# The last gate product of a transformer block, computed without two experts and completed by their own results

## The chip, the cores and the metric

The kernel runs on one core of a Trainium2 chip, in float32 throughout. The metric is the device time of one execution in microseconds; of several, the median. A core has five engines with an instruction queue each: PE (TensorE, matrix products), DVE (VectorE), ACT (ScalarE), POOL (GpSimd) and SP, which here issues nearly all transfers. Products land in PSUM banks (128 partitions x 512 floats, eight of them), from where DVE or ACT reads them.

## The reference, cut to what matters

Three layers follow each other: one with sparse attention, then two of the second block (a dense one, and one with eight experts). The change is in the last of them only. There `h` holds 256 tokens x 1024, and the tokens' router has picked two experts of eight for each:

```python
out = zeros(256, 1024)                     # the mixture of experts, e = 0..7
for e in range(8):
    out = out + combine[:, e:e+1] * ((silu(f @ w1[e]) * (f @ w3[e])) @ w2[e])
h = h + out                                # w1, w3: 1024 x 3584, w2: 3584 x 1024
gate = sigmoid(rmsnorm(h, ple_norm_g[1]) @ ple_gate_w[1])       # 1024 x 1024
h = h + gate * (p[1] @ ple_proj_w[1])                           # p: 256 x 256
```

`rmsnorm(h, g)` is h / sqrt(mean(h^2) + eps) * g. The factor of a row can therefore be applied behind the product with the gate's weights, and the product itself is linear in h.

## The kernel before, in words

Each expert has 128 places. A token that picked it stands in one of them, and the rows of a one-hot matrix (`places`, `gather`) bring its activations there, turned so that the 1024 inputs lie on partitions (`xT`). The 3584 hidden columns are cut into four chunks (`CHUNKS`: 1024, 1024, 1024, 512). A step (e, c) in `STEPS` is one chunk of one expert: product w1 (silu behind it), product w3 (multiplied to it), and behind these w2 of the *previous* step, whose result (`ys`, places x 1024) is summed over the chunks. Experts go in pairs, (0, 4), (1, 5), (2, 6), (3, 7), and the two of a pair take turns chunk by chunk. Behind an expert's last chunk its `way_back` (one-hot, turned) and `scatter` multiply the results back onto tokens and add them to `h` with the gates.

`wide` (L1467) is every such product. Weights come in parts of 128 x 1024 floats (512 KB): eight for a product of 1024 columns, four for one of 512. The first 64 places are computed part by part as the weights come, two matmuls of 64 columns side by side on PE's array for each (in the trace four records of 128x512 a part, since a float32 matmul shows as two). The further places stand under `tc.If(many() > SET)` (L1492) and are computed only if the expert has more than 64 tokens. This branch, the reading of the second bank and the release of the parts are the `rest` of a product; it is run by `catch_up` after the *first* part of the product that follows, so that PE has work queued in front of it. `mids` are pieces of other work that are put between the parts.

`_Stream` holds one list of all weights in the order in which the program takes them. Each part that is released lets SP issue the next transfer into its slot (`load`, L93). In the stage with experts there are 32 slots: 8 `raw` of pool wp, 4 `wh`, 4 `wl`, 10 `raw` of qp and 6 of rp.

At the end stand: w2(7,3), the value product p @ ple_proj_w, the scatter of expert 7 into h, the transposing of the normalised h, the test `most > CAP` (an expert with more than 128 tokens; then all experts are computed once more over a second set of places by `overflow`, which loads its weights itself), and the gate product `ple` for two token tiles of 128. Its weights are split into a high and a low part (ACT L316, DVE L320, POOL L318: `wh`, `wl`) and multiplied in three passes; the last quarter of the columns is done in pieces of 256. SP stores each piece of h. `rows`, `P`, `D` = 128, 1024; `NT` = 2 token tiles, `KD` = 8 pieces of 128 inputs, `NE` = 8, `CAP` = 128.

Of the kernel before, what the change touches and what calls it, by code (L numbers as in the profile page):

```python
# [19 lines left out]
P = 128  # L20
# [28 lines left out]
STEPS = [(e, c) for e0 in range(NE // 2) for c in range(NC) for e in (e0, e0 + NE // 2)]  # L49
# [13 lines left out]
class _Stream:  # L63
# [3 lines left out]
    def __init__(self, net, plan):  # L67
        self.net, self.plan = net, plan
        self.parts = [(i, q, s) for i, c in enumerate(plan) for q, s in enumerate(c[4])]
        self.raw, self.got = {}, {}  # L70
        self.loaded = self.opened = self.cut = self.used = self.cur = self.first = self.live = 0
        self.slots, self.cap = [(net.wp, "raw", RAW)] * RAW, RAW
        self.extra, self.hold = set(), False

        self.last, self.keep = sum(len(c[4]) for c in plan[-3:]), None
# [17 lines left out]
    def load(self, between=None):  # L93
        while self.loaded < len(self.parts) and self.loaded < self.opened + self.cap:
            slot = self.slots.pop(0)
            if len(self.parts) - self.loaded <= self.last and slot[0] is not self.keep and slot[:2] != (self.net.wp, "raw"):
                self.cap -= 1
                continue
            self.slots.append(slot)
            pool, tag, n = slot  # L100
# [17 lines left out]
    def advance(self, n=PARTS):  # L118
        stop = self.cut + n
        while self.cut < stop and self.cut < len(self.parts) and self.live < PARTS:  # L120
# [4 lines left out]
            self.net.aid = {("p", 1): (1,), ("pg", 1, 0): (0, 1, 2, 3), ("pg", 1, 1): ()}.get(self.plan[i][0], self.net.aid)  # L125
# [44 lines left out]
class _Direct:  # L170


    def __init__(self, net, stream):
        self.net = net
        self.plan = {c[0]: c for c in stream.plan}
        self.slot = (net.qp, "raw", EARLY)
        assert stream.loaded == len(stream.parts) and len(stream.parts) - stream.used <= stream.last
# [7 lines left out]
    def get(self, j):  # L185
        if j not in self.got:
            k0, k1, c0, c1 = self.parts[j]
            pool, tag, n = self.slot
            v = self.net.t(pool, [P, 1024], tag, bufs=n).rearrange("p (k n) -> p k n", k=k1 - k0)
# [4 lines left out]
    def release(self, j):  # L194
        del self.got[j]


class _Net:
# [11 lines left out]
    def weights(self):  # L210
# [22 lines left out]
        for i in range(2):  # L233
# [16 lines left out]
            else:  # L250
# [8 lines left out]
                add(("p", 1), a["ple_proj_w_2"][1], 2, D, [(0, 2, 0, 512), (0, 2, 512, D)])  # L259
            for c in range(2):  # L260
# [1109 lines left out]
    def ple(self, i, xs, x1, r, pp, out=None):  # L1370
        nc = self.nc

        def done(c):
            cs = slice(c * 512, c * 512 + 512)

            def f(t, ps, ks=slice(0, 512)):
                sg = self.t(self.act, [P, D], "x", bufs=3)[:, 0:512]
                ds = slice(c * 512 + ks.start, c * 512 + ks.stop)
                nc.scalar.activation(sg[:, ks], ps[:, ks], AF.Sigmoid, scale=r[t])  # L1379
                nc.vector.tensor_mul(sg[:, ks], sg[:, ks], pp[t][:, ds])  # L1380
                nc.vector.tensor_add(self.h[:, t, ds], self.h[:, t, ds], sg[:, ks])  # L1381
                if out is not None:
                    nc.sync.dma_start(out[:, t, ds], self.h[:, t, ds])
# [5 lines left out]
        if out is None:  # L1389
            ps = self.banks("mm")  # L1390
            return self.join(self.groups(("pg", i, 1), ps, xs, done=lambda t: f(t, ps(t)), late=False))

        parts = self.ws.take(("pg", i, 1))
        for t, c0, c1 in ((0, 0, 512), (1, 0, 256), (1, 256, 512)):
            ps = self.bank("s" if c0 else "mm")
            for n, (j, (k0, _, _, _)) in enumerate(parts):
                self.passes(ps[:, c0:c1], xs[t], self.ws.get(j), k0, n == 0, n == len(parts) - 1, slice(c0, c1))
            f(t, ps, slice(c0, c1))
# [73 lines left out]
    def wide(self, key, outs, lhs, n, many, take, mids=None):  # L1472
# [4 lines left out]
        mids = mids or {}  # L1477
        parts = self.ws.take(key)
        end = parts[-1][1][1]

        def product(s, j, k0, k1):
            w = self.ws.get(j)
# [8 lines left out]
        def rest():  # L1491
# [6 lines left out]
            for j, _ in parts:  # L1498
                self.ws.release(j)
            take(1)  # L1500

        for i, (j, (k0, k1, _, _)) in enumerate(parts):
# [5 lines left out]
            if many is None:  # L1508
                product(1, j, k0, k1)
                product(2, j, k0, k1)  # L1510
                self.ws.release(j)
# [35 lines left out]
    def down(self, key, ys, g, n, many, first):  # L1547
# [3 lines left out]
        def lhs(s, k):  # L1551
            q, r = (n // 2 // P, SUB) if s else (n // P, SET)
            return g[:, int(s > 0), q * (s == 2) + k % q, r * (k // q) : r * (k // q) + r]

# [8 lines left out]
        self.wide(key, y, lhs, 512, many, take)  # L1563
# [4 lines left out]
    def scatter(self, t, e, back, ys, many=None):  # L1568

        ps = []  # L1570
        rows = [slice(SET * j, SET * j + SET) for j in range(2)]

        def first():
            ps[:] = [self.bank("tr") for _ in range(2)]
# [9 lines left out]

        def second():
# [5 lines left out]
            for j in range(2):  # L1591
                hv = self.h[:, t, j * 512 : j * 512 + 512]
                self.nc.vector.scalar_tensor_tensor(hv, ps[j], self.gates[:, t, e : e + 1], hv, ALU.mult, ALU.add)

        return first, second

    def experts(self, sp, p):
# [22 lines left out]
        for i, (e, c) in enumerate(STEPS):  # L1620
# [14 lines left out]
            if done is not None:  # L1635
                back[done], turn = self.way_back(sp, done)
                mids.setdefault(6, []).append(turn)
                late = {2 + 2 * t + k: [f] for t in range(NT) for k, f in enumerate(self.scatter(t, done, back[done], ys[done], F(number, done)))}
            if n < 512:
                assert not late  # L1640
# [8 lines left out]
        back[done], turn = self.way_back(sp, done)  # L1649
        turn()  # L1650
        hidden(*prev)
        for t in range(NT):
            for f in self.scatter(t, done, back[done], ys[done], F(number, done)):
                f()
        x = prev[0]
        back[x], turn = self.way_back(sp, x)
        turn()
        finish(*prev[:2])
        self.catch_up()
        return [f for t in range(NT) for f in self.scatter(t, x, back[x], ys[x], F(number, x))], pT  # L1660

    def overflow(self, sp, again):

        nc = self.nc
        most = nc.values_load(self.most[0:1, 0:1], min_val=0, max_val=S)
        with self.tc.If(most > CAP):
            self.ws, self.sets = _Direct(self, self.stream), {}
            for e in range(NE):
                oh, xT, ys = self.places(sp, e, CAP), self.inputs_T(), self.results()
# [4 lines left out]
                for c in range(NC):  # L1674
                    n = CHUNKS[c][1] // 2
                    s = self.t(sp, [P, 2, 512], "sw_s")
# [3 lines left out]
                for t in range(NT):  # L1680
                    for f in self.scatter(t, e, back, ys):
                        f()
            again()
            self.ws = self.stream

    def router_inputs(self):
# [4 lines left out]
        nc.gpsimd.memset(self.zeros, 0.0)  # L1691
        self.odd = self.t(self.fp, [P, 2], "odd")
# [5 lines left out]
    def route_join(self, gen):  # L1698
# [73 lines left out]
        self.next_gain()  # L1772
# [42 lines left out]
    def moe(self, i):  # L1815
        sp = self.se
        p = self.ple_load(i, self.act, "x", 3)
        done, pT = self.experts(sp, p)
        pp = [self.t(self.act, [P, D], "x", bufs=3) for t in range(NT)]
        value = self.ple_value(i, pT, pp)  # L1820
        x0, *x0T = (self.t(self.qp, [P, D], "raw", bufs=EARLY) for _ in range(3))
        x0T = [x.bitcast(F32R).rearrange("p (k n) -> p k n", k=KD) for x in x0T]
        self.play(value, n=2)
        done[0]()
        done[1]()
        self.scaled(0, x0)
        self.play(value, n=1)
        done[2]()
        done[3]()
        self.transposed(x0, x0T, 0, 4)  # L1830
        self.play(value)
        self.transposed(x0, x0T, 4, 8)
        self.overflow(sp, lambda: self.transposed(self.scaled(0, x0), x0T))
        xs = [x0T, self.new_xT()]
# [108 lines left out]
```

## Time and profile before

| | |
|---|---|
| three executions | 1772.24, 1764.77, 1763.61 us; median 1764.77 |
| the profiled execution, its span | 1774.91 us, 1773.1 us |
| PE, its weight loads | 1652.7 us (93%), 1014.6 us (57%) |
| DVE, ACT, POOL | 671.5 us (38%), 514.1 us (29%), 158.4 us (9%) |
| transfers | 491.70 MB, mean 277 GB/s; the hardware queue 72.1% of 16 engines' span |

Busy times are of the whole span, over stages with different limits; the stage of the experts takes roughly its second half. The profiled execution lies 10.1 us above the median, so differences are taken within it. In a timeline row `[5.17 <-PEq L1492]` says that the engine stood idle for 5.17 us ahead of this row, and that the last thing to end was its own sequencer at line 1492.

### The profile page before, as it was taken

How to read it: one execution, taken by the hardware profiler on the slowest of the kernel's cores; microseconds unless marked ns; L12 is line 12 of the kernel's file. 1: busy time of each engine (PE TensorE's matmuls, PEld its weight loads, DVE VectorE, ACT ScalarE, POOL GpSimd, SP SyncE). 2: the span in 40 equal slices, each digit the busy share in tenths (PEclk: the TensorE clock that was granted, in tenths of full speed). 3: DMA queues.
4: the chain of work that ended last, by engine and by line, in shares of the span. 5: the costliest groups of instructions: out<-in, count | busy, mean ns of one | idle time of the engine just before them, and what ended most of it. 6: DMA issues, size and time to landing. Idle time of an engine off the chain costs nothing. (4 is left out here: it accounts for less than half of the span.)

```text
span 1773.1 us, 24424 instructions
## 1 busy us (share of the span) xinstructions
PE 1652.7 (93%) x9746; PEld 1014.6 (57%) x9749; DVE 671.5 (38%) x1132; ACT 514.1 (29%) x840; POOL 158.4 (9%) x152
## 2 busy tenths in 40 slices
PE   8999989999999999999997999999999998998867
PEld 6887768777888877784332534336433344333336
DVE  6656767576445587571110130101120111311134
ACT  5646646555444455551100100000000001000013
POOL 2001432510000013500000000000000000000011
PEclk9999999999999999999999999999999999998979
DMA  8654335545555558567999998999789999999951
GB/s 272 201 175 146 108 95 168 180 122 185 182 187 190 190 163 292 194 250 308 406 407 399 400 393 306 406 357 401 283 320 374 408 397 404 370 407 407 397 207 38
DMA packets 176117, 491.70 MB, mean 277 GB/s; under 512 B 16670, under 2 KB 21206, under 8 KB 175920
## 3 DMA queue, kind: packets, MB, share of 16 engines
q1 hardware_dynamic: 171376, 474.28, 72.1%
q0 software_dynamic: 4544, 14.52, 2.8%
q8 instruction: 157, 2.57, 0.6%
q14 instruction: 40, 0.33, 0.0%
HBM read 486.60 MB, written 2.14 MB: 276 GB/s over the span
## 5 line engine op out<-in xcount | busy, mean ns | idle before, releaser
L272 PE MATMUL mm<-wh,xh 128*128 128x512 f32 (+4 forms) x888 | 324.0, 432 | 7.1 <-PEq L1492 4.0
L320 DVE TENSOR_TENSOR wl<-raw,wh 128x1024 fp32r<-128x1024 f32 x211 | 266.7, 1275 | 130.8 <-ACT wh L316 120.4
L272 PE MATMUL mm<-wh,xl 128*128 128x512 f32 (+1 forms) x704 | 281.4, 400 | 0.7 <-DVE xl L491 0.5
L316 ACT CAST wh<-raw 128x1024 fp32r<-128x1024 f32 x228 | 237.5, 1051 | 143.8 <-PE mm L272 68.2
L272 PE MATMUL mm<-wl,xh 128*128 128x512 f32 (+3 forms) x924 | 254.1, 416 | 1.2 <-DVE wl L320 0.6
L272 PE MATMUL mm<-raw,xh 128*64 128x512 f32 (+3 forms) x1388 | 201.2, 467 | 20.7 <-PEq L1492 14.2
L272 PE MATMUL o<-raw,sw_g 128*64 128x512 f32 (+1 forms) x1268 | 195.5, 503 | 16.7 <-PEq L1492 9.7
L272 PE MATMUL s<-raw,xh 128*64 128x512 f32 (+3 forms) x1432 | 193.4, 457 | 16.5 <-PEq L1492 12.4
L1532 DVE TENSOR_TENSOR sw_s<-sw_s,s 128x512 f32<-128x512 f32 (+1 forms) x64 | 39.8, 621 | 405.9 <-PE s L272 367.6
L272 PEld LDWEIGHTS mm<-wh,xh 128*128 128x128 f32 (+2 forms) x888 | 145.7, 180 | 54.4 <-issue 10.6
L272 PEld LDWEIGHTS mm<-wl,xh 128*128 128x128 f32 (+2 forms) x924 | 145.1, 175 | 51.5 <-issue 10.1
L272 PEld LDWEIGHTS mm<-wh,xl 128*128 128x128 f32 x704 | 134.9, 192 | 29.8 <-DVE xl L491 2.5
L318 POOL TENSOR_TENSOR wl<-raw,wh 128x1024 fp32r<-128x1024 f32 x17 | 43.0, 2549 | 1198.4 <-ACT wh L316 1178.4
L272 PEld LDWEIGHTS s<-raw,xh 128*64 128x64 f32 (+1 forms) x1432 | 77.0, 125 | 124.2 <-issue 80.9
L1544 ACT COPY sw_g<-tr 128x512 f32<-128x512 f32 (+1 forms) x32 | 17.1, 533 | 446.9 <-PE tr L275 425.8
L272 PEld LDWEIGHTS o<-raw,sw_g 128*64 128x64 f32 (+1 forms) x1268 | 72.0, 126 | 128.8 <-issue 95.8
L272 PEld LDWEIGHTS mm<-raw,xh 128*64 128x64 f32 (+1 forms) x1388 | 72.3, 127 | 119.0 <-issue 91.8
L1557 DVE TENSOR_TENSOR xl<-xl,o 128x512 f32<-128x512 f32 x48 | 33.0, 686 | 163.3 <-PE o L272 137.2
L1530 ACT ACTIVATE sw_s<-mm 128x512 f32<-128x512 f32 (+1 forms) x64 | 34.8, 544 | 206.0 <-PE mm L272 167.8
L272 PE MATMUL o<-wh,sw_g 128*128 128x512 f32 (+2 forms) x256 | 61.0, 488 | 3.8 <-PEq L1492 2.2
L272 PE MATMUL s<-wh,xh 128*64 128x512 f32 (+6 forms) x236 | 51.0, 467 | 3.3 <-PEq L1492 2.6
L275 PEld LDWEIGHTS tr<-c_ident,sw_s 128*128 128x128 f32 x280 | 34.0, 151 | 32.8 <-issue 9.1
(363 smaller groups left out, 1606.7 us busy)
## 6 DMA issues: line engine op xcount, KB each, us to landing
raw<-in_moe_w_dram SPq DMA_DIRECT2D x504, 512.0 KB, 10.2
raw<-in_dense_w_dram SPq DMA_DIRECT2D x84, 512.0 KB, 4.5
wh<-in_moe_w_dram SPq DMA_DIRECT2D x81, 512.0 KB, 10.2
wl<-in_moe_w_dram SPq DMA_DIRECT2D x80, 512.0 KB, 10.2
raw<-in_w_in_dram SPq DMA_DIRECT2D x48, 512.0 KB, 4.6
raw<-in_nsa_w_in_dram SPq DMA_DIRECT2D x44, 512.0 KB, 5.1
raw<-in_w_o_dram SPq DMA_DIRECT2D x16, 512.0 KB, 4.8
raw<-in_ple_gate_w_dram SPq DMA_DIRECT2D x16, 512.0 KB, 5.0
```

Of the source, the lines that this page charges most:

```text
L272: self.nc.tensor.matmul(out, lhsT, rhs, start=start, stop=stop, **kw)
L275: self.nc.tensor.transpose(out, in_, self.ident if ident is None else ident)
L316: self.nc.scalar.copy(wh, v)
L318: self.nc.gpsimd.tensor_tensor(wl, v, wh.bitcast(F32), ALU.subtract)
L320: self.owed.append(lambda: self.nc.vector.tensor_sub(wl, v, wh.bitcast(F32)))
L1530: nc.scalar.activation(s[:, i, :n], ps[i][:, :n], AF.Silu)
L1532: nc.vector.tensor_mul(s[:, i, :n], s[:, i, :n], ps[i][:, :n])
L1544: copy(g[:, i, : n // P, :], ps[:, :n].rearrange("p (q n) -> p q n", n=P))
L1557: self.nc.vector.tensor_add(ys[:, i, :], ys[:, i, :], y[i])
```

## The change

Seven things change, all in the last stage:

1. *Order.* In the last pair, the steps go (3,0), (3,1), (7,0), (3,2), (3,3), (7,1), (7,2), (7,3), so that expert 3 is done three steps before the end.
2. *The store.* From w1(3,1) on, the 16 slots outside pool wp are withdrawn as they come free. Thirteen of them take p, the two pieces of ple_proj_w, the eight of ple_gate_w, and two value tiles. 16 slots stay for experts' weights.
3. *The test for overflow* (with its second pass over all experts) stands behind w2(3,0), in step (3,1), instead of at the end.
4. *The gate product without experts 3 and 7.* At step (7,0) h holds experts 0, 1, 2, 4, 5, 6. It is turned and multiplied by the gain (`gate_inputs`), the value is computed (`value_T`, `value_part`), and in steps (3,2), (3,3) and (7,1) four `gate_part`s of eight full matmuls each fill `logit` (256 x 1024).
5. *The two experts' share.* The places' results of expert 3, and at the end of expert 7, are turned, multiplied by the gain (`result_T`), passed through the gate's weights in places' order (`result_logits`, a `wide` product over resident weights), and then scattered like results, but into `logit` as well as into h.
6. *The end:* w2(7,3), `result_T`, scatter into h, `result_logits`, the sums of squares of h and the factor of each row, then four quarters: scatter into the logits (DVE), sigmoid (ACT), times value (DVE), plus h (DVE), store.
7. The splitting of the gate's weights, and the three passes, fall away for this layer.

Cut to its core:

```diff
-STEPS = [(e, c) for e0 in range(NE // 2) for c in range(NC) for e in (e0, e0 + NE // 2)]
+STEPS = [(e, c) for e0 in range(NE // 2 - 1) for c in range(NC) for e in (e0, e0 + NE // 2)]
+LAST = len(STEPS)
+STEPS += [((NE // 2 - 1, NE - 1)[j], c) for j, c in ((0, 0), (0, 1), (1, 0), (0, 2), (0, 3), (1, 1), (1, 2), (1, 3))]
...
     def load(self, between=None):
         while self.loaded < len(self.parts) and self.loaded < self.opened + self.cap:
-            slot = self.slots.pop(0)
-            if len(self.parts) - self.loaded <= self.last and slot[0] is not self.keep and slot[:2] != (self.net.wp, "raw"):
+            pool, tag, n = slot = self.slots.pop(0)
+            if self.loaded >= self.grab_at and pool is not self.net.wp:
+                if self.grab:
+                    self.grab.pop(0)(self.net.t(pool, [P, 1024], tag, bufs=n))
                 self.cap -= 1
                 continue
...
+    def gate_part(self, t, c):
+        ps = self.bank("tr")
+        for k in range(KD):
+            self.mm(ps, self.hT[t][:, k, :], self.gate_w[k][:, c * 512 : c * 512 + 512], start=k == 0, stop=k == KD - 1)
+        self.nc.scalar.copy(self.logit[t][:, c * 512 : c * 512 + 512], ps)
...
+    def result_logits(self, g, zs, many):
+        def take(i):
+            if i:
+                self.nc.vector.tensor_copy(zs[:, i, :], z[i])
+            else:
+                self.nc.scalar.copy(zs[:, i, :], z[i])
+
+        z = self.set_banks("o")
+        self.ws = _Kept(self.gate_w)
+        self.wide("gate", z, self.turned_lhs(g, 512), 512, many, take)
+        self.ws = self.stream
...
+            if i == LAST + 2:
+                for j, (t, k0) in enumerate((t, k0) for t in range(NT) for k0 in (0, 4)):
+                    mids.setdefault(3 + j, []).append(F(self.gate_inputs, t, k0))
+                late = {1: [self.value_T]}
+                for j, (t, k) in enumerate((t, k) for t in range(NT) for k in range(2)):
+                    late[3 + j] = [F(self.value_part, t, k)]
+            if i == LAST + 3:
+                mids.setdefault(5, []).append(F(self.gate_part, 0, 0))
+                late = {4: [F(self.gate_part, 0, 1)]}
+            if i == LAST + 4:
+                late = {2: [F(self.gate_part, 1, 0)]}
+            if i == LAST + 5:
+                late = {4: [F(self.gate_part, 1, 1)]}
+            if i == LAST + 6:
+                for j in range(2):
+                    mids.setdefault(4 + j, []).append(F(self.result_T, ys[done], yT[0], j))
...
+            if i == LAST + 6:
+                self.result_logits(yT[0], zs, F(number, done))
             done = finish(*prev[:2]) if prev is not None else None
             prev = (e, c, s)
-            if i == len(STEPS) - 3:
-                pT = self.ple_T(p)
+            if i == LAST + 1:
+                self.catch_up()
+
+                x, y = self.inputs_T(), self.results()
+                self.overflow(sp, x, y)
...
+        finish(*prev[:2])
+        self.result_T(ys[e], yT[1], 0)
+        self.catch_up()
+        self.result_T(ys[e], yT[1], 1)
...
+        for f in scattered(ys[e], None):
+            f()
+        self.result_logits(yT[1], zs, many)
...
+        for t in range(NT):
+            self.halves(sq[:, t], t, junk)
+        r = self.rstd(sq)
+        self.catch_up()
+        for (t, j), f in zip(((t, j) for t in range(NT) for j in range(2)), scattered(zs, self.logit)):
+            f()
+            c = slice(j * 512, j * 512 + 512)
+            sg, hv = self.t(self.wp, [P, 1024], "wl", bufs=PARTS)[:, 0:512], self.h[:, t, c]
+            nc.scalar.activation(sg, self.logit[t][:, c], AF.Sigmoid, scale=r[:, t : t + 1])
+            nc.vector.tensor_mul(sg, sg, self.value[t][:, c])
+            nc.vector.tensor_add(hv, hv, sg)
+            nc.sync.dma_start(self.out[:, t, c], hv)
```

On SP, at the end of the list of weights, before: the last parts of the experts (`in_moe_w_2_dram`), behind them the projection and the gate's weights.

```order
L89 DMA raw_16281<-in_moe_w_2_dram 128x1024
L89 DMA wh_16283<-in_moe_w_2_dram 128x1024
L89 DMA raw_16551<-in_ple_proj_w_dram 128x2x512
L89 DMA raw_16646<-in_ple_proj_w_dram 128x2x512
L1589 UNCONDITIONAL_BRANCH
L89 DMA raw_16648<-in_ple_gate_w_dram 128x2x512
L1589 UNCONDITIONAL_BRANCH
L89 DMA raw_16650<-in_ple_gate_w_dram 128x2x512
```

On SP now, in the last steps of expert 6 and expert 3: the first four of these loads (L1674 is p, L1679 are rows of the two matrices) stand among the experts' parts (L92).

```order
L92 DMA wl_14032<-in_moe_w_2_dram 128x1024
L1496 UNCONDITIONAL_BRANCH
L92 DMA raw_14034<-in_moe_w_2_dram 128x1024
L1674 DMA raw_14149<-in_p_dram 128x2x256
L1679 DMA raw_14151<-in_ple_proj_w_dram 128x1024
L1679 DMA raw_14153<-in_ple_proj_w_dram 128x1024
L1679 DMA raw_14239<-in_ple_gate_w_dram 128x1024
L1679 DMA raw_14241<-in_ple_gate_w_dram 128x1024
L92 DMA raw_14243<-in_moe_w_2_dram 128x1024
```

The eleven loads moved from behind the last part of the experts to ahead of its last 144 parts.

On PE now, in product w3 of step (3,2): `s_6883` is the bank of the first 64 places, `wh` and `wl` are the experts' parts; the rows on `tr_25389` are a `gate_part` with the resident weights `raw_14239` to `raw_14548`.

```order
L1496 UNCONDITIONAL_BRANCH
L287 MATMUL s_6883<-wh_25245,xh_13949 64x512 x2
L287 MATMUL s_6883<-wh_25247,xh_13949 64x512 x2
L287 MATMUL s_6883<-wh_25249,xh_13949 64x512 x2
L287 MATMUL tr_25389<-raw_14239,xh_14995 128x512
L287 MATMUL tr_25389<-raw_14241,xh_14995 128x512
...
L287 MATMUL tr_25389<-raw_14548,xh_14995 128x512
L287 MATMUL s_6883<-wl_25251,xh_13949 64x512 x2
L287 MATMUL s_6883<-wl_25253,xh_13949 64x512 x2
```

Eight matmuls over all 128 tokens of a tile stand between two parts of an expert's product, whose release comes after them.

On DVE now, at the end: a sum of the factor's steps (`rms`), the copy of the second bank of `result_logits`, and of the four quarters the first two.

```order
L447 SCALAR_TENSOR_TENSOR rms_y_3239_27072<-rms_z_3238_27071,rms_y_3239_27072 128x2
L1658 COPY x_26136<-o_7222 128x512
L1781 UNCONDITIONAL_BRANCH
L1596 SCALAR_TENSOR_TENSOR x_24885<-tr_27151,gates_6842,x_24885 128x512
L1800 TENSOR_TENSOR wl_27177<-wl_27177,raw_14155 128x512
L1801 TENSOR_TENSOR h_85<-h_85,wl_27177 128x512
L1596 SCALAR_TENSOR_TENSOR x_24885<-tr_27152,gates_6842,x_24885 128x512
L1800 TENSOR_TENSOR wl_27183<-wl_27183,raw_14155 128x512
L1801 TENSOR_TENSOR h_85<-h_85,wl_27183 128x512
```

Each quarter's scatter add (L1596) stands behind the product and the add of the quarter ahead of it (L1800, L1801), of which the product waits for ACT's sigmoid.

## Rows read from the trace of the kernel before

**Rows 1.** Windows: core, busy time and records of each engine, granted clock, transfers.

```profile
core 0: us, PE busy (x) PEld busy (x) DVE busy (x) ACT busy (x) POOL busy (x), PEclk, DMA share, GB/s
1550.00:1598.00 48.00, 45.49 (x212) 17.18 (x210) 5.51 (x8) 4.73 (x8) 0.00 (x0) 1.00 1.03 407
1598.00:1704.00 106.00, 83.54 (x403) 34.78 (x399) 13.13 (x21) 6.64 (x13) 0.00 (x0) 0.89 1.02 397
1704.00:1726.00 22.00, 15.76 (x42) 6.16 (x40) 10.60 (x21) 3.21 (x4) 4.65 (x2) 0.60 0.23 83
```

**Rows 2.** Waits of the queue that issues weights: total us, times, longest.

```profile
SPq L89 <- DMA raw<-in_moe_w_dram: 90.7, 100, 1.5
```

**Rows 3.** Timeline of PE, 1560 to 1598 us: start, length, work, records, idle ahead.

```profile
1560.26 6.23 PE L272 MATMUL s<-raw,xh 128*64 128x512 f32 x28 [0.16 <-PEq L1492]
1575.12 1.06 PE L272 MATMUL mm<-raw,xh 128*64 128x512 f32 x4
1598.01 1.36 PE L272 MATMUL mm<-raw,xh 128*64 128x512 f32 x4
```

**Rows 4.** Timeline of PE, the long gaps of three steps after 1598 us.

```profile
1601.57 1.63 PE L272 MATMUL mm<-raw,xh 128*64 128x512 f32 x4 [2.19 <-PEq L1492]
1632.16 1.98 PE L272 MATMUL mm<-raw,xh 128*64 128x512 f32 x4 [5.14 <-PEq L1492]
1664.67 1.94 PE L275 MATMUL tr<-c_ident,sw_s 128*128 128x128 f32 x8 [5.17 <-PEq L1492]
```

**Rows 5.** Timeline of SP: last part of an expert, first gate weights.

```profile
1688.56 0.33 SPq L89 DMA_DIRECT2D wh<-in_moe_w_dram  x1
1694.66 33.88 SPq L89 DMA_DIRECT2D raw<-in_ple_gate_w_dram  x8
```

**Rows 6.** Transfers issued from 1550 us on: count, KB each, us to landing.

```profile
raw<-in_moe_w_dram SPq DMA_DIRECT2D x109, 512.0 KB, 10.2
```

**Rows 7.** Timeline of PE, from the last w2 on.

```profile
1720.45 4.96 PE L272 MATMUL o<-raw,sw_g 128*64 128x512 f32 x12
1725.24 1.02 PE L272 MATMUL o<-wh,sw_g 128*64 128x512 f32 x4
1740.84 0.49 PE L272 MATMUL mm<-wh,raw 128*128 128x512 f32 x1 [3.06 <-ACTq L1666]
```

**Rows 8.** Timeline of PE, 1496 to 1553 us: gather, scatter, start of w1, transposes.

```profile
1496.15 2.05 PE L272 MATMUL tr<-oh,f 128*128 128x128 f32 x16
1534.45 1.13 PE L272 MATMUL tr<-xl,back 64*128 64x512 f32 x4
1550.63 1.06 PE L272 MATMUL mm<-wh,xh 128*64 128x512 f32 x4
1552.85 1.09 PE L275 MATMUL tr<-c_ident,sw_s 128*128 128x128 f32 x8
```

**Rows 9.** Groups by line and form, 1726 to 1773 us.

```profile
L1593 DVE SCALAR_TENSOR_TENSOR h<-tr,gates,h 128x512 f32<-128x512 f32 x4 | 2.8, 742 | 2.8 <-PEq L1589 2.8
L1381 DVE TENSOR_TENSOR h<-h,x 128x512 f32<-128x512 f32 x3 | 2.1, 691 | 0.1
L1379 ACT ACTIVATE x<-mm,rms_k 128x512 f32<-128x512 f32 x3 | 2.1, 690 | 4.3 <-PE mm L272 4.3
L1557 DVE TENSOR_TENSOR xl<-xl,o 128x512 f32<-128x512 f32 x2 | 1.4, 684 | 4.3 <-PE o L272 4.3
```

**Rows 10.** Timeline of ACT and DVE in the end.

```profile
1743.24 0.61 ACT L436 ACTIVATE raw<-h 128x512 f32<-128x512 f32 x1
1743.98 0.21 DVE L447 TENSOR_SCALAR rms_v<-rms_q 128x1 f32<-128x1 f32 x1
1745.73 0.16 DVE L432 SCALAR_TENSOR_TENSOR rms_k<-rms_z,rms_k 128x1 f32<-128x1 f32 x1
1769.78 0.42 DVE L1381 TENSOR_TENSOR h<-h,x 128x256 f32<-128x256 f32 x1
```

More of the change, by code (lines that the diff above doesn't have):

```diff
@@ L73, in __init__ @@
         self.extra, self.hold = set(), False
-        self.last, self.keep = sum(len(c[4]) for c in plan[-3:]), None
+        self.grab = []
+        self.grab_at = next(u for u, (i, _, _) in enumerate(self.parts) if plan[i][0] == ("w1", *STEPS[LAST + 1]))
     def whole(self, u):
@@ L195, in release, with __init__, take, get @@
         del self.got[j]
+class _Kept:
+    def __init__(self, tiles):
+        self.tiles = tiles
+    def take(self, key):
+        return [(k, (k, k + 1, 0, D)) for k in range(len(self.tiles))]
+    def get(self, j):
+        return self.tiles[j].rearrange("p (k n) -> p k n", k=1)
+    def release(self, j):
+        pass
 class _Net:
@@ L1388, in ple @@
         f = done(1)
[L1389 to L1398, printed above, removed]
+        ps = self.banks("mm")
+        return self.join(self.groups(("pg", i, 1), ps, xs, done=lambda t: f(t, ps(t)), late=False))
     def where(self, pos, t, e):
@@ L1591, in second, with gate_inputs @@
             for j in range(2):
[L1592 to L1597, printed above, removed]
+                add(j)
+        return first, second, others, add
+    def gate_inputs(self, t, k0):
+        ps = self.bank("tr")
+        for k in range(4):
+            self.tp(ps[:, k * P : k * P + P], self.h[:, t, (k0 + k) * P : (k0 + k + 1) * P])
+        g = self.gT[:, k0 : k0 + 4].unsqueeze(2).to_broadcast([P, 4, P])
+        self.nc.vector.tensor_mul(self.hT[t][:, k0 : k0 + 4, :], ps.rearrange("p (k n) -> p k n", k=4), g)
@@ L1648, in experts @@
+        nc, many = self.nc, F(number, e)
+        back[e], turn = self.way_back(sp, e)
+        turn()
         self.catch_up()
-        back[done], turn = self.way_back(sp, done)
-        turn()
         hidden(*prev)
-        for t in range(NT):
[L1653 to L1658, printed above, removed]
-        self.catch_up()
-        return [f for t in range(NT) for f in self.scatter(t, x, back[x], ys[x], F(number, x))], pT
@@ L1662, in overflow, with scattered @@
-    def overflow(self, sp, again):
+        finish(*prev[:2])
+        self.result_T(ys[e], yT[1], 0)
+        self.catch_up()
+        self.result_T(ys[e], yT[1], 1)
+        self.sets.pop("mm")
+        def scattered(ys, to):
+            steps = [self.scatter(t, e, back[e], ys, None, to, ("tr", "mm")[t]) for t in range(NT)]
+            for f in steps:
+                f[0]()
+            with self.tc.If(many() > SET):
+                for f in steps:
+                    f[2]()
+            return [F(f[3], j) for f in steps for j in range(2)]
@@ L1815, in moe @@
     def moe(self, i):
[L1816 to L1834, printed above, removed]
-        x1 = self.scaled(1, self.t(self.rp, [P, NT, D], "f")[:, 1, :])
-        sq = self.sq_tile()
-        self.halves(sq[:, 0], 0, x0)
-        self.ple(i, xs, x1, [self.factor(sq)], pp, self.out)
+        self.reserve(i)
+        self.experts(self.se)
     def run(self, stop):
```

116 lines of the change are left out of this document (81 added, 35 removed).

## The prediction

> **What bounds the kernel now.** I read first the windows of the last 290 us, then the waits of the queue that issues the weights, then the matmul engine's order of time, and last the steps after the final weights. In the windows [rows 1] the reader is to see the change of regime: up to 1704 us the transfers are full (share 1.02, 397 GB/s) while PE is busy 83.5 of 106 us; after 1704 they fall to 83 GB/s, and what is left is a chain of PE, DVE and ACT. SP agrees: 100 of its issues waited for an earlier weight transfer, 90.7 us together [rows 2]. A part (512 KB) at 407 GB/s costs 1.29 us of transfer.
>
> PE needs less for a part. 28 records are 7 parts; 6.23 us less some 0.25 us for the last result make 0.854 us a part. A plain step of 24 parts takes PE 22.89 us (1575.12 to 1598.01) against 24 x 1.29 = 31.0 us of transfers [rows 3]. So PE works off a backlog until 1598 and then waits for weights. It waits in an odd way: one gap of 2.19, 5.14 and 5.17 us a step, put down to its own sequencer at the branch behind w2 (PEq L1492), and then many parts without a wait [rows 4]. With work queued the same branch costs 0.16 us, in the first row of that group [rows 3].
>
> Before, the last expert part is issued at 1688.56 us [rows 5] and lands about 10.2 us later [rows 6], near 1699; PE is done with it only at 1725.24 + 1.02 = 1726.3 [rows 7], and the span ends at 1773.1: an end of 46.8 us that holds the gate product.
>
> **The change part by part.**
>
> *Transfers.* The same bytes, in another order: 10 parts of gate and projection weights and 0.25 MB of p now come ahead of the last 144 expert parts. 5.5 MB at 405 GB/s is 13.6 us, so the last expert part could land at 1699 + 13.6 = 1712. The store shrinks from 32 parts to 16, two products of 8: a product's transfers can start when the one two places ahead has been given back.
>
> *PE, added inside the stream.* No row shows a whole-array fp32 matmul of 512 columns. Bounds: 8 of 128 columns took 2.05 us [rows 8], so at most 4 x 0.256 = 1.02 us; at least 0.427 us, half of a pair of 64-column ones, if two could share the array as those do. The pair itself streams 512 columns in 0.854, which I take. Then: gate_part 4 x 8 x 0.854 = 27.3; value_part 8 x 0.854 = 6.8; 28 transposes at 1.09 us for 8 [rows 8] = 3.8; result_logits of expert 3, 8 x 0.854 = 6.8; its way back 0.9 (six transposes at 1.09 us for 8, and the start), its scatter into h and then into the logits 4 x 1.13 [rows 8] = 4.5. Together 50.1 us.
>
> *The check for overflow* moves to 1550 us. All engines jump over the code of a whole expert loop; before, PE stood 3.06 us there [rows 7]. The transfers were then quiet, and now they are full, where smaller jumps cost 5.17 against 2.19. Bounds 3 and 10 us; I take 6. SP must also see its eight transfers landed before it goes on, some 3 us without transfers. PE holds 16 landed parts (two products, 14 us of work) meanwhile, so that costs nothing; without this cover it would be 3 us.
>
> *Sum for PE.* Up to 1550.63 [rows 8] PE does the same work as before (the gather of expert 7 only goes from one step to the next). From there to the end of the last w2: 128 parts x 0.854 = 109.3; 19 products with 0.43 us each for branch and start (22.89 - 24 x 0.854 - 1.09, by three) = 8.2; transposes of the hidden values 5 x 1.09 + 2 x 0.6 = 6.6; added 50.1; way back of expert 7, 0.9; check 6; two waits for a bank's copy, 1.4. Sum 182.5, so 1733.1. The transfers need until 1712 + 3 + some 1.5 = 1717. PE has become the bound of these steps, and the end of the experts comes 6.8 us later than 1726.3. The transfers keep ahead, though with little: 182.5 us over 16 products is 11.4 us each, against 8 x 1.29 = 10.3 and about 2 us to restart.
>
> *The new end*, by its order: DVE adds the first bank 0.8 [rows 9]; four transposes 0.65; branch and second bank 1.5; four transposes 0.75; scatter into h, two pairs, 2.1; gate product of expert 7, 8 x 0.854 + 0.25 = 7.1; ACT copies 0.65; then ACT, in its order behind that copy, squares h, four times 0.61 [rows 10] with 0.3 for the last read-out and the hand-over = 2.7; the factor, 11 small DVE steps where 8 took 1.92 us (1743.98 to 1745.89) [rows 10], 2.5; DVE copies 0.7. Then four quarters in DVE's order, each add, sigmoid on ACT, product, add: 0.70 + 0.69 + 0.69 + 0.69 and the hand-overs = 2.85 [rows 9], together 11.4, none beside another, since the next quarter's first add stands behind this one's last. Out and finish 2.9 (1770.2 to 1773.1) [rows 10]. Sum 33.8. To this I add 1.5 us for PE at the lower clock in part of it: after its gaps in 1704 to 1726 the granted clock was 0.60 [rows 1], and 3 parts took 4.96 us, 1.65 each [rows 7]. The bound above is 8 x 0.8 = 6.4, below nothing.
>
> The old split of the gate weights on ACT, DVE and POOL goes; it was beside PE and brings nothing of its own.
>
> **Sum.** 1733.1 + 33.8 + 1.5 = 1768.4 against the span of 1773.1: 4.7 us less, 1774.91 to 1770.2 for the profiled execution. The median of the runs, 1764.77, lies 10.1 below that execution; with the same difference it becomes 1760.
>
> **The rivals.**
>
> *The added PE work hides.* PE was idle 22.5 of the 106 us before 1704 [rows 1]; if its sum is 16 us shorter than mine, the transfers still bound and the experts end at 1717. The end is then 1717 + 35.3 = 1752.3, 20.8 less: 1744. Against it: 50 us added, and the steps up to 1598 had next to no idle time (45.5 of 48 us busy).
>
> *The small store lets PE run dry: slower.* Each gate_part (6.8 us) holds back the release of a product. If transfers then restart late, PE catches up with them, stands at every branch behind w2 with nothing queued, and pays what it paid after 1598: the mean of 2.19, 5.14 and 5.17, 4.2 us. Five such places make 21 us: 1781. It turns the sign at two, and is slower by more than 0.5% from four. For it: 2 us to restart is my guess, the median of 10.2 us being mostly queue [rows 6]; against it: PE has more to do than the transfers. [...]
>
> *The closing product at the lower clock.* Then the end has 6.4 and not 1.5 us of it: 1765, still no change. For it: PE has four gaps of 0.7 to 1.5 us just ahead. [...]
>
> **How the numbers follow.** Forecast 0.56, its own range 1752 to 1770; hidden 0.13; dry 0.17; lower clock 0.14. What this kernel's measurement can tell is about 0.5%, 8.8 us: 1756 and 1773.6. Faster: the hidden case 0.13, and 0.17 of the forecast where the matmul or the check is cheaper than taken; slower: the dry case 0.17, and 0.02 of the others. The range reaches to most of both outer cases: 1746 to 1778.
>
> **What would show it.** PE's steps from 1555 on without gaps over 1 us and the last w2 ending near 1733 show the sum right; an earlier end with PE waiting for weights shows the first rival, gaps of 3 to 5 us at the branch behind w2 the second. A gate_part should take 6.8 us. The end from the last w2 should be 34 to 36 us, with DVE at 2.85 us a quarter. Wrong would be: weights landing after PE wants them in most products, a check that costs over 10 us, or an end over 40 us.

## The result and the profile after

The changed kernel took 1789.4 us, median of 4 runs (1786.4 to 1791.2), beside 1768.5 of the kernel before (its three executions and a fourth of 1774.75): a ratio of 1.0114, interval 1.0073 to 1.0155. A second comparison gave 1784.1, ratio 1.0088 (1.0059 to 1.0118). It is slower by 16 to 21 us; the forecast was 1760, a gain of 4.7, and the range 1746 to 1778.

In what follows *stream* is the stretch from the end of the second w2 of the last pair (the third step; in the first profile of the kernel before this w2 ends at 1550.8 us, just behind the start of the next product in [rows 8]) to the end of the last w2, and *end* what comes after it. The first profile of the kernel before lay at the upper end of its runs; a second one (span 1765.9) stands beside it.

| profile | third step begins | stream | end |
|---|---|---|---|
| before, first and second | 1550.8, 1547.0 | 175.4, 172.8 | 46.8, 46.2 |
| forecast | 1550.6 | 182.5 | 35.3 |
| changed, first and second | 1539.1, 1539.5 | 212.7, 206.9 | 37.2, 35.5 |

The end came as forecast. The stream took 24 to 30 us more than its sum. That the third step begins some 10 us earlier was not forecast; the last run below shows that the change doesn't explain it. The windows of the changed kernel, with the same columns as [rows 1]:

```profile
core 0: us, PE busy (x) PEld busy (x) DVE busy (x) ACT busy (x) POOL busy (x), PEclk, DMA share, GB/s
1539.00:1598.00 59.00, 51.70 (x196) 18.87 (x196) 7.59 (x11) 6.46 (x11) 0.00 (x0) 0.94 0.83 324
1598.00:1650.00 52.00, 47.32 (x204) 19.88 (x202) 3.60 (x6) 4.30 (x8) 0.00 (x0) 0.93 0.86 323
1650.00:1700.00 50.00, 48.30 (x202) 16.67 (x198) 13.09 (x23) 3.93 (x7) 0.00 (x0) 1.00 0.97 376
1700.00:1752.00 52.00, 42.91 (x198) 16.77 (x198) 11.75 (x22) 2.31 (x5) 0.00 (x0) 0.87 0.58 217
1752.00:1789.00 37.00, 16.46 (x56) 5.83 (x56) 15.88 (x33) 7.20 (x14) 0.00 (x0) 0.74 0.08 30
```

Transfers ran at 324 and 323 GB/s up to 1650 us, where they had 407 before [rows 1]; PE was busy 99 of 111 us. PE is now what bounds, as the sum had it. The reader finds the lost time in PE's own order of time, changed kernel:

```profile
1545.97 3.68 PE L287 MATMUL mm<-wh,xh 128*64 128x512 f32 x8 [6.83 <-PEq L1809]
...
1588.85 7.13 PE L287 MATMUL tr<-raw,xh 128*128 128x512 f32 x16
...
1599.73 2.80 PE L287 MATMUL s<-wh,xh 128*64 128x512 f32 x12 [0.16 <-PEq L1496]
...
1630.98 1.12 PE L287 MATMUL s<-wl,xh 128*64 128x256 f32 x3 [3.89 <-issue]
1632.02 9.44 PE L287 MATMUL tr<-raw,xl 128*128 128x512 f32 x16
...
1702.35 9.20 PE L287 MATMUL o<-raw,xh 128*64 128x512 f32 x28 [2.96 <-PEq L1496]
...
1729.88 1.97 PE L287 MATMUL s<-wh,xh 128*64 128x256 f32 x8 [3.29 <-PEq L1602]
...
1748.17 3.65 PE L287 MATMUL o<-raw,sw_g 128*64 128x512 f32 x16
```

A gate_part takes 7.13 us (6.8 were taken), and 16 gaps of the stream behind branches are of 0.15 or 0.16 us. But PE stands 6.83 us at the check, and 3.89, 2.96 and 3.29 us at three other places, each within a few records behind a skipped branch, once in the middle of a part of weights (five of its eight records had run), once in result_logits, whose weights stay in place: neither can be a wait for weights. "issue" means that the profile shows nothing PE waited for. Behind the gap of 3.89 us a gate_part took 9.44 us for 7.13, and in the first 5 us the granted clock was 0.50:

```profile
1630.90:1636.00 5.10, 5.02 (x8) 2.14 (x9) 0.00 (x0) 0.00 (x0) 0.00 (x0) 0.50 1.03 407
```

The second profile has the same four at the same instructions (7.03, 3.61, 2.85, 3.58 us).

What the gaps have beside them is the queue named `instruction`. Its row, 1505 to 1720 us, of the changed kernel and then of the second profile before (packets, MB, share; which engine a packet is for isn't shown):

```profile
q8 instruction: 28, 0.46, 0.8%
```

```profile
q8 instruction: 31, 0.51, 1.0%
```

0.46 MB in 28 packets are 16 KB each. Theory A began as: PE is the bound, and loses time at jumps over code and at the lower clock behind them. With these rows I gave it a mechanism, a guess of mine that no row shows: behind a jump over much code PE waits for a packet of this queue.

### The profile page after: what moved, and what is told of

Same layout as the page of the kernel before. It is cut to its first block, busy times and chain, and to the rows that moved or that the text cites. A ratio compares the mean times of both kernels' runs of the same rounds, so it can differ in the third digit from the quotient of the medians.

```text
span 1789.0 us, 24489 instructions
## 1 busy us (share of the span) xinstructions
PE 1670.9 (93%) x9778; PEld 1001.4 (56%) x9781; DVE 670.6 (37%) x1131; ACT 504.8 (28%) x831; POOL 144.0 (8%) x146
## 5 line engine op out<-in xcount | busy, mean ns | idle before, releaser
L287 PE MATMUL mm<-wh,xh 128*128 128x512 f32 (+3 forms) x888 | 317.4, 433 | 13.1 <-PEq L1809 6.8
L287 PE MATMUL mm<-wh,xl 128*128 128x512 f32 x680 | 271.2, 399 | 1.0 <-DVE xl L506 0.9
L331 ACT CAST wh<-raw 128x1024 fp32r<-128x1024 f32 x218 | 227.0, 1049 | 128.6 <-PE mm L287 66.6
L287 PE MATMUL mm<-raw,xh 128*64 128x512 f32 (+3 forms) x1340 | 185.8, 456 | 8.8 <-PEq L1496 6.7
L287 PE MATMUL o<-raw,sw_g 128*64 128x512 f32 (+1 forms) x1228 | 182.6, 496 | 10.8 <-PEq L1496 8.3
L287 PE MATMUL s<-raw,xh 128*64 128x512 f32 (+3 forms) x1344 | 176.9, 453 | 12.6 <-PEq L1496 9.8
L287 PEld LDWEIGHTS s<-raw,xh 128*64 128x64 f32 (+1 forms) x1344 | 69.2, 124 | 111.6 <-issue 76.8
L287 PE MATMUL s<-wh,xh 128*64 128x512 f32 (+5 forms) x292 | 62.9, 493 | 5.2 <-PEq L1602 3.8
L333 POOL TENSOR_TENSOR wl<-raw,wh 128x1024 fp32r<-128x1024 f32 x12 | 30.3, 2554 | 324.4 <-ACT wh L331 304.4
L287 PE MATMUL o<-wl,sw_g 128*64 128x512 f32 (+2 forms) x224 | 51.9, 515 | 3.6 <-DMA wl<-in_moe_w_dram 1.5
```

Source lines behind the costliest of these rows:

```text
L287: self.nc.tensor.matmul(out, lhsT, rhs, start=start, stop=stop, **kw)
L331: self.nc.scalar.copy(wh, v)
L333: self.nc.gpsimd.tensor_tensor(wl, v, wh.bitcast(F32), ALU.subtract)
```

## The experiments

**The changed kernel again, and without the check.** The second takes out one line:

```diff
-                self.overflow(sp, x, y)
```

> The changed kernel once more, beside the others on the same chip. Theory A (PE is the bound from the third step of the last pair on, and loses time at jumps over code and at the lower clock behind them): 1789 us, ratio 1.011; the stalls of PE stand at the same instructions as in the first profile: some 6.8 us at the check, 3.9 us in w3(3,3), 3.0 us in result_logits of expert 3, 3.3 us at the scatter in w3(7,3). Theory B (the store of 16 parts is too small and PE waits for weights): the stalls move from run to run with the transfers.

> The changed kernel without the test for overflow and the second pass behind it (left out: places past 128, which no expert has here). Theory A: the stall of 6.8 us and some 2.4 us of lower clock behind it go, so 1780 us, 9 less than the changed kernel. Theory B: PE has landed parts in front of it there, and the transfers' pause of the check goes too: 3 less. Theory C (the check alone makes the change slower, since it stops PE and the transfers together): 20 less, 1768.

1784.1 us, with the stalls at the same instructions; and 1778.3 us, ratio to before 1.0057 (1.0034 to 1.0081). The check is worth 6 to 11 us, of which theory A gave 9 (6 in the same comparison, with intervals that overlap); theory C falls, and so does B's claim that stalls move about from run to run. The check isn't the whole of it: without it the other three places still stall, for 4.68, 0.86 and 2.52 us, and two more do (1.00 and 2.66).

**Without the branches of experts 3 and 7,** in the changed kernel and in the kernel before:

```diff
-            with self.tc.If(many() > SET):
...
+            if many is not FEW:
+                with self.tc.If(many() > SET):
...
+        few = lambda e: FEW if e in (3, 7) else F(number, e)
```

> The changed kernel without the branches of experts 3 and 7 for places past 64 (left out: that code, which is jumped over here since both have at most 64 tokens). Theory A: the stalls of 3.9, 3.0 and 3.3 us go, with some 6 us of lower clock behind them and 0.2 us at each of 23 other branches: 1789 - 16 to 20 = 1771. Theory B: they were waits for weights, and stand elsewhere: at most 4 less.

> The kernel before, without the branches of experts 3 and 7 for places past 64 (left out: that code). Its gaps at L1492 in the last pair (2.2, 5.1, 5.2, 3.4 us) I had read as waits for weights. Theory A (stalls at jumps cost the changed kernel 30 us since it has made PE the bound there; before, the transfers bound and hid most of them): 5 to 10 less than before, 1760. Theory D (jumps cost both kernels the same, and the change is slower for another reason): 30 less, 1738. If the gaps were weights: no change, and the gaps stay.

1754.5 us (ratio 0.9911, 0.9882 to 0.9941), some 30 us less than the changed kernel, and 1745.0 us (0.9890, 0.9832 to 0.9948), 24.6 less than before. More than theory A gave on both sides: by the medians, jumps cost the kernel before nearly as much, so theory D is half right. Instruction packets, the same row for the changed kernel and the kernel before, without the branches:

```profile
q8 instruction: 10, 0.16, 0.3%
```

Ten each. In the changed kernel without branches the check is the only gap in the stream that PE's sequencer or "issue" ends, and it costs 2.73 us instead of 6.83 (windows, then PE's timeline):

```profile
1600.00:1650.00 50.00, 50.00 (x235) 20.25 (x234) 5.04 (x9) 4.46 (x9) 0.00 (x0) 1.00 0.96 369
1650.00:1700.00 50.00, 49.31 (x246) 18.26 (x246) 14.85 (x26) 4.09 (x8) 0.00 (x0) 1.00 1.01 393
```

```profile
1541.99 1.94 PE L288 MATMUL mm<-wh,xh 128*64 128x512 f32 x8 [2.73 <-PEq L1809]
...
1591.02 3.60 PE L288 MATMUL s<-wh,xh 128*64 128x512 f32 x16
1594.55 7.13 PE L288 MATMUL tr<-raw,xh 128*128 128x512 f32 x16
```

Its stream is 181.0 us, beside 182.5 in my sum. PE has the same 792 records with and without the branches (793 in one profile), and this is what they took (the two streams of the changed kernel, then the one without branches):

```profile
1539.14:1751.82 212.68, 190.09 (x792) 72.19 (x792) 35.90 (x61) 17.00 (x31) 0.00 (x0) 0.94 0.81 310
1539.46:1746.40 206.94, 184.22 (x793) 70.31 (x792) 35.90 (x61) 17.00 (x31) 0.00 (x0) 0.97 0.83 318
1539.26:1720.30 181.04, 175.82 (x792) 66.60 (x792) 34.32 (x60) 16.37 (x31) 0.00 (x0) 0.99 0.89 345
```

Of the 28.8 us between the mean of the first two and the third, 17.4 are idle time and 11.3 longer busy time for the same work. The kernel before without branches shows what its stream is bound by (PE's timeline, and a window):

```profile
1588.14 1.08 PE L273 MATMUL s<-raw,xh 128*64 128x512 f32 x4 [0.20 <-DMA raw<-in_moe_w_dram]
1589.42 1.08 PE L273 MATMUL s<-raw,xh 128*64 128x512 f32 x4 [0.20 <-DMA raw<-in_moe_w_dram]
1590.70 1.08 PE L273 MATMUL s<-raw,xh 128*64 128x512 f32 x4 [0.20 <-DMA raw<-in_moe_w_dram]
```

```profile
1600.00:1650.00 50.00, 43.40 (x208) 12.18 (x204) 6.68 (x11) 3.50 (x7) 0.00 (x0) 1.00 1.03 404
```

Each part takes 1.28 us, of which 0.20 is a wait for its transfer; transfers are full. Its stream is 159.2 us, so the branches cost 14.9 of the 174.1 (mean of two), with stalls such as these in the second profile before:

```profile
1597.03 1.08 PE L272 MATMUL mm<-raw,xh 128*64 128x512 f32 x4 [1.52 <-PEq L1492]
...
1659.18 1.94 PE L275 MATMUL tr<-c_ident,sw_s 128*128 128x128 f32 x8 [5.19 <-PEq L1492]
...
1682.67 4.28 PE L272 MATMUL mm<-raw,xh 128*64 128x256 f32 x22 [3.51 <-issue]
```

Those 5.19 us answer to the 5.17 of [rows 4]. I had read the gaps there as waits for weights; weights are waited for in pieces of 0.20. (The 24.6 us of the medians are more than 14.9: in its profile this kernel also begins the third step 15 us earlier than the mean of the two before, for which see the last run.)

**With the inner branch left out only.**

```diff
-                with self.tc.If(many() > SET + SUB):
-                    ...
+                if key[1] not in (3, 7) and key != "gate":
+                    with self.tc.If(many() > SET + SUB):
+                        ...
```

> The changed kernel, where experts 3 and 7 keep the branch for places past 64 but not the inner one for places past 96 (left out: that inner code, half of what is jumped over). Theory A, with code fetched in packets as its mechanism: about half of the instruction packets between 1550 and 1720 us that the branchless kernel saved (21 against 6) go, and half of the 30 us: 1769. If a jump costs the same whatever it jumps over: at most 5 less than the changed kernel's 1784.

1770.9 us (ratio 0.9997, 0.9973 to 1.0022), 13 to 18 less, with 20 packets instead of 28:

```profile
q8 instruction: 20, 0.33, 0.6%
```

The stream is 195.0 us, 14.9 of the 28.8 less: half the code, half the cost, with the same number of outer branches. But the stalls didn't become half as long. The three of 3 to 4 us are gone; what is left is the check, and nothing longer than 0.72 us:

```profile
1543.19 3.68 PE L287 MATMUL mm<-wh,xh 128*64 128x512 f32 x8 [6.91 <-PEq L1810]
...
1711.58 1.08 PE L287 MATMUL s<-wh,xh 128*64 128x256 f32 x8 [0.72 <-PEq L1603]
```

So whether such stalls come here depends on the length of the skipped code. That the price grows in proportion to it isn't shown: with a quarter of the code (below) the stream is 196.4 us, no shorter. What remains above 181.0 are the check, the gaps of 0.16 us, and the products that each branch cuts in two (a w2 of eight parts takes 7.22 us from start to start in the changed kernel, 6.86 without its branch).

**Less gate work, and a larger store.**

```diff
-        for k in range(KD):
+        for k in range(1):
```

> The changed kernel with one matmul of eight in each gate_part (left out: 28 of 32 matmuls of the early gate product). Theory A: PE is the bound, so all of it is seen: 28 x 0.89 = 25 less, 1764. Theory B: PE waits for weights in their place: at most 8 less.

```diff
-            if self.loaded >= self.grab_at and pool is not self.net.wp:
+            if self.loaded >= self.grab_at and pool is not self.net.wp and self.grab:
...
-                            + [rows(self.gate_w, a["ple_gate_w_2"][i], k) for k in range(KD)])
+                            + [rows(self.gate_w, a["ple_gate_w_2"][i], 0)])
```

> The changed kernel with one row tile of the gate's weights instead of eight (left out: seven of the eight rows, 3.7 MB), so that 26 parts stay in the store instead of 16. Theory B (the small store lets PE run dry): 10 to 20 less than the changed kernel, 1765 to 1775. Theory A (PE is the bound, its stalls are its own code): at most 5 less, with the stalls of 3 to 7 us still there.

1783.0 us (ratio 1.0078, 1.0048 to 1.0108) and 1785.9 (1.0095, 1.0066 to 1.0124): neither gains anything. The first is a miss of theory A. PE's timeline and a window of it:

```profile
1612.23 1.08 PE L287 MATMUL o<-raw,sw_g 128*64 128x512 f32 x4 [0.18 <-DMA raw<-in_moe_w_dram]
...
1634.17 8.94 PE L287 MATMUL o<-raw,sw_g 128*64 128x512 f32 x28 [6.20 <-issue]
...
1684.05 1.97 PE L287 MATMUL s<-raw,xh 128*64 128x512 f32 x3 [3.50 <-issue]
```

```profile
1600.00:1650.00 50.00, 38.86 (x186) 13.07 (x184) 5.40 (x9) 3.48 (x7) 0.00 (x0) 0.93 0.98 377
```

With 25 us less to do PE comes up to the transfers (0.18 us of wait for a part, as above), has no queue of landed parts, and stalls longer: 6.20 and 3.50 us, with others of 1.2 to 1.7, and one of 4.37 that a weight transfer ends. With the larger store three of the four stalls still stand there (7.47, 2.77, 2.88 us; 0.80 at the fourth) and no time is gained, so theory B falls.

**Both at once:** no branches of experts 3 and 7, and one matmul of eight.

> The changed kernel without the branches of experts 3 and 7, and with one matmul of eight in each gate_part (left out: that code, and 28 of 32 matmuls of the early gate product). With the branches in, leaving out the 28 matmuls gained nothing. Theory E (the added work fills PE beyond what the transfers leave free; in that run the stalls and the transfers' pauses had eaten what the matmuls gave): without stalls the 25 us of PE work are worth what PE lies above the transfers, 8 to 14: 1743. Theory F (the added work is hidden beside the transfers, and the 9 us are lost elsewhere): at most 3 less than 1754.

1739.1 us (ratio 0.9805, 0.9748 to 0.9863), 15.3 less than without branches alone, or 19 by the ratios, since in this comparison the kernel before took 1775.3: theory E. Its stream is 164.7 us beside 181.0 with all the gate work and 159.2 of the kernel before, and its transfers are full:

```profile
1600.00:1650.00 50.00, 45.59 (x212) 13.34 (x208) 8.72 (x18) 3.88 (x8) 0.00 (x0) 1.00 1.03 409
```

**Another order in the end** (squares and factor ahead of `result_logits`; a quarter's add ahead of the product before it):

```diff
+        logits(0)
+        for q, (t, c) in enumerate(quarters):
+            if q + 1 < len(quarters):
+                logits(q + 1)
```

> The changed kernel with another order in its end, all work kept: the sums of squares and the factor ahead of result_logits instead of behind ACT's copy, and the four quarters shifted against each other, so that the next quarter's add into the logits stands ahead of this one's product. 4 us for the factor and 3 us for the quarters: 7 less than the changed kernel, 1777, if the end is the chain that the profile shows; no change if ACT and DVE only move the wait.

1782.3 us (1.0077, 1.0052 to 1.0102): 2 to 7 less, with overlapping intervals, so the median shows no clear gain. In the profile the end takes 31.0 us instead of 35.5 and 37.2. The chain of the changed kernel, and then of this one (start, length, what):

```profile
1774.45 0.67 DVE x L1596
...
1775.14 0.73 ACT wl L1799
...
1775.90 0.70 DVE wl L1800
...
1776.62 0.06 DVE h L1801
...
1777.23 0.75 DVE x L1596
```

```profile
1775.80 0.74 DVE x L1596
1776.55 0.61 DVE wl L1809
...
1777.18 0.04 DVE h L1810
...
1777.79 0.74 DVE x L1596
```

A quarter takes 2.78 us there and 1.99 here, since ACT's 0.73 has left the chain.

**Short code that keeps all work.** Places past 64 become one set of 64 behind one branch, 16 matmuls in place of 64:

```diff
-                    product(1, j, k0, k1)
-                with self.tc.If(many() > SET + SUB):
-                    for j, (k0, k1, _, _) in parts:
-                        product(2, j, k0, k1)
+                    product(3 if one else 1, j, k0, k1)
+                if not one:
+                    ...
```

> The kernel before, all work kept, with the places past 64 of experts 3 and 7 as one set of 64 behind one branch, in place of two sets of 32 behind two: 16 matmuls stand behind a product's branch instead of 64, so a quarter of the code is jumped over. Theory A (the stalls are code that PE fetches, and grow with what it jumps over): instruction packets between 1505 and 1720 us fall from 31 to about 15, and three quarters of the 24.6 us that leaving the code out gave come back: 1751. If what costs is the number of branches: 10 less at most, 1759.

> The changed kernel with the same short code for experts 3 and 7, and the order of the end of a_tail. Theory A: three quarters of the 30 us, and 3 us of the end: 1759, still 8 behind the kernel before with the same code, since the gate work then fills PE up to the end while the transfers would be done earlier. Rival (with short code the change shows its gain): below the kernel before with that code.

> The kernel before with one set of 64 for all eight experts. Where an expert has 65 to 96 tokens a product's further part then costs PE as much as its first (7.1 us for eight parts instead of 3.7). Theory A: steps 8 to 20, with further places, get longer by 3 us a product, steps of experts with under 64 tokens shorter; sum over 1751, probably near 1780.

> The changed kernel with the order of the end of a_tail and one set of 64 for all eight experts, beside the kernel before with it (1738). Theory E: the last pair stays bound by PE, so it keeps its 7 to 10 us behind: 1746. Rival (the earlier steps end with a larger backlog of landed weights, and the change gains): 1735.

| kernel | experts 3 and 7 | all experts |
|---|---|---|
| before, short code | 1753.0 (0.9916, 0.9887 to 0.9945) | 1738.2 (0.9827, 0.9777 to 0.9877) |
| changed, short code, new end | 1760.1 (0.9940, 0.9916 to 0.9963) | 1749.9 (0.9873, 0.9820 to 0.9926) |

The first column came within 2 us of what theory A gave. In the kernel before, the stream fell to 159.5 us, so all of the 14.9 came back, with 14 packets from 1505 to 1720 us for the 15 expected and no gap over 0.3 us that PE's sequencer ends. In the changed kernel it fell to 196.4, of which the check takes 7.1; its match with 1759 is luck in part, since it also reached the third step 10 us earlier than the changed kernel, which nothing had forecast. For all experts I expected a loss of PE time, and it gained 15 us more: packets between 820 and 1690 us are 103 with short code for two experts and 51 for all; that stalls of the earlier steps went with them is my inference. The changed kernel stays 7 us behind in the first column, and 8 (by the ratios) to 12 (by the medians) in the second, whose rows come from two comparisons; the intervals of a column overlap. The kernel before with short code for all experts is the fastest version that keeps all work.

**The kernel before once more.**

> The kernel before once more, for a second profile: its first one was an execution of 1774.9 us, at the upper end of its runs, and reached the last pair of experts 14 to 16 us later than the nine profiles of other kernels with the same code ahead of it. Expected: it gets there near 1510 us, and from there to the end it takes 250 to 257 us.

A span of 1765.9 us; the third step begins at 1547.0 and the rest takes 219.0. The point was not reached near 1510: my expectation missed. All kernels with the change's order begin the third step at 1525 to 1542 us, the kernel before twice near 1549. But the kernel before without branches, which has the old order, begins it at 1533.6. The difference is there already at the first product of the last pair, ahead of all the work on PE that the change moves (kernel before, changed kernel):

```profile
1489.03 1.06 PE L272 MATMUL mm<-raw,xh 128*64 128x512 f32 x4
```

```profile
1477.09 1.06 PE L287 MATMUL mm<-raw,xh 128*64 128x512 f32 x4
```

| profile | first product of the last pair | from there to the end |
|---|---|---|
| before, first and second | 1489.0, 1485.4 | 284.1, 280.5 |
| changed, first and second | 1477.1, 1477.6 | 311.9, 304.3 |
| before, changed, both without branches | 1473.4, 1479.5 | 266.2, 278.4 |
| before, changed, short code for 3 and 7 | 1486.2, 1467.8 | 267.5, 288.9 |
| before, changed, short code for all | 1478.8, 1465.2 | 267.9, 285.6 |

So the order of the steps isn't what gives it, and its cause stays open. Counted from the last pair on, the change costs some 26 us and not 16 to 21, 12 without the branches, and 21 and 18 with short code (mostly one profile each).

## Why the prediction failed, step by step

- *Transfers.* Right in kind: full in the kernel before, and no longer the bound after the change.
- *PE's added work.* Nearly right: 7.13 us a gate_part (6.8), 1.98 a value_part (1.7). Without branches the stream is 181.0 us with a check of 2.7 in it; my terms without the check, and with 0.2 us for each product's start, come to 172, so some 6 us were left out. A likely place are the starts of pieces put between others: a part alone takes 1.01 us from start to start, one in a row 0.86. That 181.0 lies so near my 182.5, which has branches and a check of 6 in it, is chance.
- *Branches.* This is the step that failed: "19 products with 0.43 us each for branch and start", taken from a stretch that had just 0.16 us behind a branch [rows 3]. Without the 0.2 us of a start they are 4.4 us, and with the check 10.4. Measured, branches and check cost 31.5: the changed kernel's streams (mean 209.8) lie 28.8 us above the one without branches, whose check takes 2.7. These 21 us and the 6 left out above are the 27 by which the stream was longer than its sum. The row just ahead of that stretch, with landed weights behind it, would have told against the 0.16 us (kernel before):

```profile
1569.09 6.23 PE L272 MATMUL o<-raw,sw_g 128*64 128x512 f32 x28 [1.75 <-PEq L1492]
```

I had the gaps of 2.19, 5.14 and 5.17 us in [rows 4] before me, with PE's sequencer as what ended them, and put them down to a queue without work.
- *The check.* 6.83 and 7.03 us for 6, and some 1 to 3 us of slower work behind it (3.68 and 3.26 us for the two parts that take 1.94 without branches; in the first profile the granted clock was 0.50 from 1545.9 to 1551.0 us).
- *What the branches cost on either side.* PE's gaps that its sequencer or "issue" ends add up to nearly the same in both kernels: 20.1 and 16.8 us in the streams before, 19.5 and 19.6 in those after. Before, 14.9 are paid, all as idle time; the busy time is the same with and without the branches (142.4 us). In the changed kernel PE is the bound and pays 28.8: 17.4 idle, and 11.3 of longer busy time. Together with 21.8 us of work that PE can't hide (181.0 - 159.2) that is 35.7 more in the stream (209.8 - 174.1); 10.1 less in the end (36.4 for 46.5), and 9.6 of an earlier start leave 16.0, which is the difference of the mean spans (1785.5 - 1769.5). The forecast had 6.8 for the stream, and took the start as unchanged: those 9.6 us came by luck, and without them the change would lose some 26.
- *The end.* 37.2 and 35.5 for 35.3 us; a quarter 2.8 to 2.9 as forecast; result_logits takes 1.4 us more in the first profile (8.5 for 7.1, at a mean granted clock of 0.83) and nothing more in the second (7.1).
- *The rivals.* "PE runs dry" had the sign and the place of the loss, stalls behind branches, but its mechanism is wrong: they come in the middle of a part and in a product over weights that stay in place, and a larger store gains nothing. It had five places of 4.2 us; there are three of 3 to 4 us, the check (6.83), 16 gaps of 0.15 or 0.16 us and 11 us of longer busy time. Rows of 0.16 us and of 3 to 7 us behind branches stand side by side; no run here shows what decides at one branch which of them comes.

That the skipped code makes the stalls is shown: they go when it is left out, halved or cut to a quarter, with the branches in place in the last two. That a stall waits for an instruction packet is inferred, from the packets (10, 20 and 28: 1754, 1771, 1784 to 1789 us) and from "issue" gaps where no weights were wanted; no row joins one packet to one stall.

## What to carry to other kernels

Look at how much code a skipped branch jumps over, and count instruction packets: a gap that a sequencer or "issue" ends, a few records behind a branch, need not be a wait for data. Here, with 64 matmuls behind the branch of a product, PE stalled for 1 to 5 us at some of the branches; with 32 or 16 it stalled for 0.7 us at most, the check apart. Work moved into a stream that transfers bind is free only up to where the engine becomes the bound; from there that work costs (without branches, leaving out 25 us of gate work took 16.3 us off the stream: 181.0 to 164.7), and so do slow matmuls behind a stall (11.3 us here). Compare profiles from the first point that the change touches: here a difference of some 10 us lay ahead of it. Before moving work, take away the stalls: short code behind rare branches gave some 31 us here (ratio 0.983), where the change lost 16 to 21.

## What the runs showed of the hardware

After 3.89 us of gap a gate_part took 9.44 us instead of 7.13, and the granted clock was 0.50 for the first 5 us behind it. Work behind a stall wasn't always slower: in result_logits the 28 records behind 2.96 us of gap took 9.20 us in the first profile, at a mean granted clock of 0.67, and 6.23 behind 2.85 us in the second, as with the larger store behind 2.88 us and with the other end behind 2.94. The same check costs 6.8 to 7.5 us in eight profiles, two of them with short code ahead of it (7.1 and 7.2), and 2.73 and 2.43 us in the two where the branches ahead of it were gone, though the code behind it is the same. Why isn't known.
